# A new written order for the closing part of an RWKV-7 layer, with one more wait, and a few places changed in the order at the layer boundary

## The chip, the cores and the metric

The kernel runs on one core of one Trainium2 chip. A core has five engines with instruction queues of their own: TensorE (PE: matrix products into PSUM banks, and the loading of weights ahead of each, PEld), VectorE (DVE), ScalarE (ACT), GpSimd (POOL) and SyncE (SP), which here issues the DMA transfers. Engines wait for each other through semaphores; within an engine, instructions go in the order in which they were written into its queue. The metric is the device time of one execution in microseconds (us); lower is better. Times of before: 786.66, 784.89 and 787.54, with a median of 786.66.

## The reference, cut to what matters

One inference step of a two-layer decoder trunk with width 1024, run for a prompt of 512 tokens and for a sample group of 8 sequences of 4 tokens, 544 columns in all. Layer one mixes tokens with dilated windowed attention, layer two with RWKV-7 (12 heads of 64); each also attends to 256 memory tokens. The branches are joined, multiplied by a SiLU gate, and projected back to width 1024; the result is normalized (RMSNorm) and added to the layer's input. Of layer two:

```python
def mixer_b(xn, w_in, w_out, mu, w0, w_up, a0, a_up, k_k, k_a, r_k, ln_w, ln_b, mem_kv, shift_prev, s0):
    p = xn @ w_in
    cols = p[..., :C_SHIFT]
    ...
    xs = (cols + mu * (prev - cols)).astype(jnp.float32)
    w_log = -jax.nn.softplus(-(w0 + jnp.tanh(wd) @ w_up)) - 0.5
    decay = jnp.exp(-jnp.exp(w_log))
    a = jax.nn.sigmoid(a0 + ad @ a_up)
    ...
    y, S = wkv_scan(r, decay, k, v, -kk, kk * a, s0)
    mean = jnp.mean(y, axis=-1, keepdims=True)
    var = jnp.mean(jnp.square(y - mean), axis=-1, keepdims=True)
    y = (y - mean) * lax.rsqrt(var + GN_EPS) * ln_w.reshape(RWKV_HEADS, HEAD_DIM) + ln_b.reshape(RWKV_HEADS, HEAD_DIM)
    y = y + jnp.sum(r * k * r_k, axis=-1, keepdims=True) * v
    ...
    o_mem = cross_attn(q_mem, mem_kv)
    h = jnp.concatenate([y, o_mem], axis=-1) * jax.nn.silu(gate)
    return h @ w_out, cols[:, -1], S.astype(xn.dtype)
...
    sa = jnp.einsum('bhvk,bhk->bhv', S, a_t)
    S = S * w_t[:, :, None, :] + sa[..., None] * b_t[:, :, None, :] + v_t[..., None] * k_t[:, :, None, :]
    return S, jnp.einsum('bhvk,bhk->bhv', S, r_t)
...
        xp = xp + rms_norm(hp, norm_post[i])
        xs = xs + rms_norm(hs, norm_post[i])
```

The second function above is one step of the scan per head, and the last two lines stand around each layer. `r`, `k`, `v`, `wd` and `ad` are columns of `xs`. Beside the outputs of the trunk the kernel returns the new memory keys and values, rows of the windows, the states `S` and the shifted columns.

## The kernel before, in words

**Tiling.** All weights come from HBM in pieces of 256 KB. Products keep float32 accuracy by splitting each operand into a high and a low part and doing three matmuls for each product: high by high, high by low, low by high (L336 to L338 for input products, L1941 for output products). So each weight piece means one DMA issued on SP's queue, one cast on ACT for the high part (L328) and one subtraction on POOL for the low part (L329), ahead of its matmuls.

**The recurrence.** The 12 heads are handled as six pairs, and these as three groups of two pairs (g = 0, 1, 2). The 512 prompt tokens are cut into 8 chunks of 64. Within a chunk the recurrence needs the inverse of a triangular matrix. A forward elimination on DVE makes it for a group at once: 30 steps of two instructions each, a product (L1557) and an addition (L1559), on fewer columns from one step to the next. At two places (after steps 12 and 22) PE multiplies a finished square (L1541) and DVE copies it back, which the following steps need. A big transposition on DVE (L1569), two matmul groups on PE (X1 at L1579, X2 at L1589) and the products w (L1600) and q/v (L1615) then make the inputs of the chunks. The chunks of a group run one after another (class `Chunks`): `inputs` (PE with the state, then one DVE addition, L1795, then POOL scales the state, L1799) and `state` (PE, then one DVE addition that writes the new state St, L1812, or for the first a copy, L1814). Each such DVE instruction counts as one step of the chain; its number is kept in `n`, and the instructions in the list `ops`. `y_of` (L1757) makes the outputs y of two chunks in one PSUM bank: a first half (`e` is 1) without the two terms that depend on the second chunk's state, and a second half with the rest. [...]

**The closing part.** Up to some point, the order of all work comes from a planner (class `Flow`): each strand of work is a Python generator (a stream) with a rank, and `run` picks the stream to go on, by costs and due times. When the event "closing" comes, `close` (L231) takes over: it walks the string CLOSE (L57), and each word in it runs the named stream up to its next `yield`. This is done within a region with a manual schedule for PE, DVE, ACT and POOL: those four engines issue their instructions in the order written. SP's queue of DMA issues is not bound by it, nor is the place at which the first instructions of the region come among earlier ones on their engine. The streams are:

- F, `earlier`: the output projection of groups 0 and 1, two output halves each. Blocks of 128 tokens by 512 columns, six matmuls (L1941) in a PSUM bank from a pool of two that other work uses as well, then the addition to z on DVE (L2134). Block and addition are separate words, and the first words of a stream may only pass its events: counted from 0, F #3 is the first block that the list places and F #4 the first addition. A sample block (L1950, named o110s for group 1's second half) and its addition (zS, L2139) close each half. The blocks of group 1's second half are o110 t0 to t3.
- W: the weight pieces of these blocks and of group 2's.
- P2: the rest of the elimination of group 2, steps 8 to 30, the two squares (words P2 #6 and #17), transposition and products.
- W1: the group norm of group 1 held back until here: its matmul sums, POOL's statistics, the scaling yc (L1642, word #3), the matmul gn (L1648).
- R, `residuals` (L1983 to L2008): loads of x and of the norm's weights (R #2), then eight transposes of x on PE into the same pool of banks (L2001) with a copy on ACT (L2002), and the sample's (x1s).
- U, `inner`: the gating of group 1's heads (`gated`, k = 2, 3): one DVE instruction over 544 columns (L1929), casts on ACT (L1932), the low part on POOL (L1933).
- C, `chunks`: state and inputs of group 2's chunks; with the count of steps above there are 15 (state of chunk 0 is step 1, inputs 1 step 2, and so on).
- Y, `outputs` (its loop has `i` from 0 to 7): the calls of `y_of`. The stream yields at the events that it needs; a word is spent at each.
- N0 to N2: the group norms of the three blocks of y of group 2 (chunks 0 to 3, 4 and 5, 6 and 7; YB), with their gating; S2 and M2: the sample's chunk for group 2 (with the product q2s, L1682, and w2s and zs4 later) and its norm (M2 #1 is a power on POOL, L1640, and gn2s its matmul).
- O0 to O3, `last`: output blocks of group 2 for 128 tokens each (two blocks, additions, a square on ACT that sums up), the power on POOL, two products with the norm's weights (L2040, on POOL or DVE by the string MULT 'GGGGGGDD': POOL for O0 to O2, DVE for O3), two last additions of x with the store (L2045).
- L, `last_sample` (L2064 to L2078): the same for the sample, with a matmul sss (L2069) that sums over the partitions.

**The boundary.** Between layer one and layer two, the string PROGS (L35) gives by letters the order of PE's work in three patterns, each in a region with a manual schedule for PE alone (L1141): p is a part of layer one's last output product, P one of layer two's first products (L336 to L338), w and W are weight pieces of the output and of the memory, I the memory's input, r, a, A, b, B parts of the norm (powers and statistics), e early work, s sums of squares (ssz L1055, L1102), x loads of the layer's input, m memory keys and values, and k (`busy`, L1133) two matmuls of 128x128 whose result nobody reads, so PE only spends time with it.

Of the kernel before, what the change touches and what calls it, by code (L numbers as in the profile page):

```python
# [13 lines left out]
SYNC = DependencyInfo(DependencyClass.Sync, DependencyReason.DATA)  # L14
# [17 lines left out]
ET = mybir.EngineType  # L32
D, A, G = ET.DVE, ET.Activation, ET.Pool
MENG = set(), set(), set()
PROGS = ('xpxwpxpwpxPxwPwPsPxPxsxsWsswkPPWsWIPsWs', 'xrxxPWrPIsWxPrsWPrsxWaakxaPasabxsbIPxbaaaPPssbbIsbb', 'brermrkAArAmBBBAmBmABAmBmABmmAmBme')  # L35
LOP = (0, 3, 4)
WOB = 10
DU = 2
# [15 lines left out]
PRELOAD = ()  # L54
MULT = 'GGGGGGDD'
LOWER = 'GGGGGG'
CLOSE = 'F F F W1 W1 W1 P2 P2 P2 P2 F P2 P2 P2 F P2 R R F F W W P2 F F P2 F F P2 F F P2 P2 R W P2 W1 P2 R R F W1 W1 U U U W W P2 R F P2 F P2 U U P2 F P2 F P2 F F P2 W W F P2 F W F F R P2 F F P2 W W P2 F F P2 F F F P2 P2 F P2 P2 P2 P2 W W P2 F P2 P2 C C C F C C S2 S2 S2 F F Y Y Y Y C Y Y Y C W F C C Y Y W W F C Y Y Y N0 N0 C N0 F C F F Y Y Y N0 F C C Y Y Y N0 N1 N1 C F N0 N1 F C N0 N0 N1 F N1 C N1 Y Y Y F F N0 N0 N0 C C N1 N1 Y Y Y S2 N2 N2 O0 O0 O0 N1 N2 S2 O1 O1 O1 O0 N2 O1 S2 O0 N1 N1 S2 S2 O1 O0 O0 O1 S2 O2 O2 O2 S2 N2 O2 O1 O0 O0 S2 O2 O2 O0 O0 O1 O1 S2 S2 O1 O1 R M2 R N2 O2 N2 N2 R N2 R R N2 N2 M2 O2 O1 C O2 O0 O2 O2 M2 M2 L L L L O3 O3 O3 O3 O1 O1 O3 O3 L L O2 O2 O2 O3 O3 O3 L L O3 O3 L C C L L L O0 O0 O3 O3 O3 L L'  # L57
YB = [[[0, 4], [4, 8]], [[0, 4], [4, 8]], [[0, 4], [4, 6], [6, 8]]]
QUARTERS = (1, 1), (0, 0), (1, 0), (0, 1)
QO = (0, 2, 1, 3)  # L60
# [194 lines left out]
def _device(tc, I, O):  # L255
# [456 lines left out]
    with ExitStack() as pro:  # L712
# [44 lines left out]
        for j, g in enumerate(GORD):  # L757
            a = 1152 + 32 * j
# [259 lines left out]
    half = {}  # L1018
# [107 lines left out]
    def busy():  # L1126

        n = 0
        while True:
            pt = ps_q(f"busy{n}")  # L1130
            n += 1
            for _ in range(2):
# [7 lines left out]
             "e": early(), "k": busy(), "s": sums(), "x": x_in()}  # L1140
    for k, prog in enumerate(PROGS):  # L1141
        with tc.manual_schedule(engines={ET.PE} | MENG[k]) if MENG[k] is not None else ExitStack():
# [65 lines left out]
    flow = Flow(tc)  # L1208
# [97 lines left out]
    def turned(c, j, h):  # L1306
        return h ^ (c + j) % 2
# [438 lines left out]
    class Chunks:  # L1746

        def __init__(self, g):
            self.g, self.st = g, sts[g]
            self.states, self.c, self.yps, self.norms, self.fence, self.n, self.ops = [], 0, None, [], False, 0, []  # L1750
            self.St = rw.tile([128, 2, 64], F32, tag="St", bufs=4, name=f"St{g}i")
            nc.vector.memset(self.St, 0.0)
            self.states.append(self.St)
            self.zs = ps_zs(f"z{g}").rearrange("p (e k c v) -> p e k c v", k=2, c=4, v=64)
# [5 lines left out]
        def y_of(self, cs, e):  # L1760


            g, (AR, SR, UV, u) = self.g, (self.st.AR, self.st.SR, self.st.UV, self.st.u)
            a, b = [ab for ab in YB[g] if ab[0] <= cs[0] < ab[1]][0]
            if cs[0] == a and e:
                self.yps = ps_c("y", f"y{g}_{a}")
            yps = self.yps
            steps = [(c, k, t) for c in cs for k in range(3) for t in range(2) if (c or k) and (k == 0 and t) == e]
            for step in steps:
                c, k, t = step  # L1770
                for j, h in PAIRS:
                    if turned(c, j, h) == t:
                        r, s = score(c, j, h)
                        lhs = SR[r, 2 - k, j, s] if k else AR[H2[h], j, 1, CH[c]]
                        rhs = (UV[r, 1, j, unit(c, j, h)[1]] if k == 1 else u[r, c, t] if k else self.states[c][H2[h], j ^ h])
                        y = ((c - a) * 2 + h) * 64
                        self.put(yps[r, y:y + 64], lhs, rhs, e and step == steps[0], not e and step == steps[-1])
                        if not e and self.fence:
                            tc.add_manual_dep(flow.last(), self.ops[self.begun if g == 2 else -1].name, SYNC, reason="one half of a bank")
            c = cs[1]  # L1780
            if not e and c == b - 1:
                def out(pt):
                    pt = pt[:, 0:(b - a) * 128].rearrange("p (c j t) -> p c j t", j=2, t=64)
                    for j in range(2):
                        add_affine(2 * g + j, pt[:, :, j], slice(64 * a, 64 * b), True)

                self.norms.append(norm(g, yps, 2 * (b - a), f"_{b}", out, self.fence))
# [306 lines left out]
    def closing():  # L2094
# [65 lines left out]
        def outputs():  # L2160
            yield "chunks"
            C = out.chunks
            for i in range(8):
                c = i + 1
                yield f"step{2 * c - 2 + c % 2}"
                if i % 2:
                    yield f"step{n + 1}"
                else:
                    if [i] == [b for _, b in YB[2] if b == i]:
                        yield f"read{i}"  # L2170
                n = C.n
                if c % 2:
                    C.begun = n
                C.y_of((c - 1, c) if c % 2 else (c - 2, c - 1), c % 2 == 1)
                flow.done(f"turn{i}")
                yield
# [125 lines left out]
```

## Time and profile before

| | us |
|---|---|
| median of three runs | 786.66 |
| the profiled execution, its own time | 787.78 |
| its span, from the first to the last instruction | 785.9 |
| the first output block of the list CLOSE on PE (F #3) | starts at 690.03 |
| the second-level transposition on DVE (L1569) | starts at 714.55 |
| the last block-sized matmul on PE | ends at 775.57 |

The mean granted clock of TensorE in this execution is 0.986 of the full one. The page of the profile gives the busy time of each engine over the whole span and where the span's final chain ran. Its tables by stage (busy time in a stretch between two times, with the granted clock), the list of waits (engine, tile and line that waited, on what, the sum, how often, the longest) and single instructions in order of time (start, duration, engine, line, operation, out<-in; in brackets the idle time just before and what ended it) are where the numbers of the prediction come from. All starts are us from the first instruction of the span.

### The profile page before, as it was taken

The page shows a single profiled execution, that of the slowest core. Times are in us where ns is not written, and L with a number is a line of the kernel's source. Part 1 is how long each engine was busy: PE and PEld are TensorE (multiplying, and loading weights), DVE is VectorE, ACT ScalarE, POOL GpSimd, SP SyncE. Part 2 cuts the span into 40 slices and gives each one's busy share as a digit, 9 for nine tenths or more (in the row PEclk, how much of TensorE's full clock was granted, in tenths as well). Part 3 has the DMA queues.
Part 4 walks back from the last instruction along what each step waited for, and adds up shares of the span by engine and source line. Part 5 has one row for each costly group of instructions (what it writes and reads, how often), then busy time and mean ns, then how long its engine had stood idle before and what let it go on. Part 6 is the DMA issues. An engine that isn't in the chain of part 4 may idle for free.

```text
span 785.9 us, 20504 instructions
## 1 busy us (share of the span) xinstructions
PE 744.5 (95%) x8457; PEld 622.5 (79%) x8457; DVE 448.0 (57%) x1076; ACT 342.0 (44%) x807; POOL 354.4 (45%) x385
## 2 busy tenths in 40 slices
PE   6899999999999999999999999999999999989894
PEld 5877868888986877798888889888897888657763
DVE  7733321216646376662444679644799457777566
ACT  7554321214554364447585358223644242533122
POOL 4642322332240393655443338533855444333465
PEclk9999999999999999999999999899999999999997
DMA  7465358872133772263114522201222341622003
GB/s 254 126 204 200 108 172 278 318 279 98 63 116 117 250 233 75 69 198 103 54 49 148 166 80 80 71 16 33 80 73 83 112 112 56 185 93 84 17 15 132
DMA packets 58785, 98.21 MB, mean 125 GB/s; under 512 B 7775, under 2 KB 23039, under 8 KB 58655
## 3 DMA queue, kind: packets, MB, share of 16 engines
q1 hardware_dynamic: 58692, 96.91, 37.7%
q8 instruction: 66, 1.08, 0.6%
q14 instruction: 27, 0.22, 0.1%
HBM read 83.39 MB, written 13.49 MB: 123 GB/s over the span
## 4 chain that ended last, share of the span: by engine, by line
PE 67%; DVE 15%; POOL 5%; DMA 5%; ACT 3%; issue 3%; SPq 0%; DVEq 0%; POOLq 0%; ACTq 0%
PE o L1941 3%; PE Sx L591 2%; PE b_h L337 2%; PE y L1757 2%; PE b_h L336 2%; PE b_h L338 2%; DVE TX L1557 1%; PE z L1757 1%; PE sc L1473 1%; PE ox L615 1%; DMA raw_a<-in_w_in_a 1%; PE o L832 1%; PE ptx L607 1%; DVE T L1559 1%; PE w L1600 1%
## 5 line engine op out<-in xcount | busy, mean ns | idle before, releaser
L329 POOL TENSOR_TENSOR lo_a<-raw_a,hi_a 128x512 fp32r<-128x512 f32 x44 | 56.9, 1295 | 124.1 <-ACT hi_a L328 123.4
L329 POOL TENSOR_TENSOR lo_b<-raw_b,hi_b 128x512 fp32r<-128x512 f32 x58 | 78.5, 1354 | 73.4 <-ACT hi_b L328 62.4
L328 ACT CAST hi_a<-raw_a 128x512 fp32r<-128x512 f32 x44 | 27.3, 620 | 64.3 <-DMA raw_a<-in_w_in_a 36.5
L328 ACT CAST hi_b<-raw_b 128x512 fp32r<-128x512 f32 x58 | 36.4, 628 | 31.8 <-issue 9.9
L336 PE MATMUL b_h<-xg,hi_b 128*128 128x272 f32 x160 | 47.9, 300 | 0.0
L337 PE MATMUL b_h<-xg,lo_b 128*128 128x272 f32 x160 | 47.2, 296 | 0.0
L338 PE MATMUL b_h<-xg,hi_b 128*128 128x272 f32 x160 | 47.1, 295 | 0.0
L1941 PE MATMUL o<-hi_o,h 128*128 128x512 f32 x96 | 36.0, 426 | 2.9 <-DVE z L2134 2.3
L337 PEld LDWEIGHTS b_h<-xg,lo_b 128*128 128x128 f32 x160 | 30.1, 188 | 2.3 <-issue 1.9
L1559 DVE TENSOR_TENSOR T<-T,TX 128x30 f32<-128x30 f32 (+14 forms) x90 | 30.1, 335 | 2.2
L336 PEld LDWEIGHTS b_h<-xg,hi_b 128*128 128x128 f32 x160 | 30.1, 188 | 1.3 <-ACT hi_b L328 0.4
L1557 DVE TENSOR_TENSOR TX<-T,TT 128x30 f32<-128x30 f32 (+14 forms) x90 | 29.2, 325 | 3.3 <-ACT T L1528 1.7
L338 PEld LDWEIGHTS b_h<-xg,hi_b 128*128 128x128 f32 x160 | 30.1, 188 | 0.9 <-issue 0.5
L1941 PEld LDWEIGHTS o<-hi_o,h 128*128 128x128 f32 x96 | 18.8, 196 | 9.3 <-DVE z L2134 2.8
L329 POOL TENSOR_TENSOR lo_o<-raw_o,hi_o 128x512 fp32r<-128x512 f32 x12 | 15.7, 1316 | 22.1 <-ACT hi_o L328 14.8
L1799 POOL TENSOR_TENSOR Sd<-St,DF 128x128 f32<-128x128 f32 x21 | 8.9, 422 | 36.6 <-DVE St L1812 25.0
L1941 PE MATMUL o<-lo_o,h 128*128 128x512 f32 x48 | 19.7, 411 | 0.9 <-POOL lo_o L329 0.9
L1382 POOL TENSOR_TENSOR rv<-rv,mhalf 128x10 f32<-128x10 f32 x6 | 14.2, 2374 | 13.8 <-DVE rv L1381 7.7
L1473 PE MATMUL sc<-AR,BK 64*64 64x128 f32 x384 | 18.4, 278 | 1.9 <-DVE bv L1419 0.9
L824 ACT COPY PT<-pa 128x512 f32<-128x512 f32 x16 | 9.0, 586 | 18.7 <-PE pa L823 14.7
L1933 POOL TENSOR_TENSOR h<-ug,h 128x128 fp32r<-128x128 f32 (+3 forms) x11 | 9.1, 838 | 17.1 <-ACT h L1932 17.0
L1473 PEld LDWEIGHTS sc<-AR,BK 64*64 64x64 f32 x384 | 12.6, 132 | 5.2 <-issue 1.8
(1112 smaller groups left out, 2732.3 us busy)
## 6 DMA issues: line engine op xcount, KB each, us to landing
raw_b<-in_w_in_b SPq DMA_DIRECT2D x58, 256.0 KB, 2.9
raw_a<-in_w_in_a SPq DMA_DIRECT2D x44, 256.0 KB, 2.9
kc<-in_kc SPq DMA_DIRECT2D x18, 512.0 KB, 6.3
vc<-in_vc SPq DMA_DIRECT2D x18, 512.0 KB, 6.9
raw_o<-in_w_out_b SPq DMA_DIRECT2D x16, 256.0 KB, 2.6
out_win<-t SPq DMA_DIRECT2D x12, 272.0 KB, 3.4
x<-in_x SPq DMA_DIRECT2D x8, 272.0 KB, 5.2
xr<-in_x SPq DMA_DIRECT2D x16, 136.0 KB, 4.1
```

Source lines behind the costliest of these rows:

```text
L328: nc.scalar.copy(hi, raw)
L329: lo_eng.tensor_tensor(lo, raw, hi.bitcast(F32), ALU.subtract)
L336: nc.tensor.matmul(ps[:, :n], hi, xh, start=first, stop=False)
L337: nc.tensor.matmul(ps[:, :n], lo, xh, start=False, stop=False)
L338: nc.tensor.matmul(ps[:, :n], hi, xl, start=False, stop=last)
L591: nc.tensor.matmul(S[hh][64 * e:64 * e + 64, 0:256], qm[r, f, a:a + 64], kT[l][r, f, :], start=True, stop=True)
L1382: nc.gpsimd.tensor_tensor(rv[:, 1], rv[:, 0], mhalf.to_broadcast([128, 10]), ALU.pow)
L1473: nc.tensor.matmul(pts[e][unit(c, j, h)[0], a:a + 128], BK[H2[h], j, x, CH[c]], AR[H2[h], j, :, CH[c]], start=True, stop=True)
L1557: nc.vector.tensor_tensor(pd, TP[:, 0:s, s:s + 1].to_broadcast([128, s, w]), TT[:, s:s + 1, s + 1:32].to_broadcast([128, s, w]), ALU.mult)
L1559: nc.vector.tensor_tensor(TP[:, 0:s, s + 1:32], TP[:, 0:s, s + 1:32], pd, ALU.add)
L1757: nc.tensor.matmul(out, lhs, rhs, start=start, stop=stop)
L1941: nc.tensor.matmul(ps, x, w, start=begun is None and i + k == 0, stop=i == len(hs) - 1 and k == 2)
```

## The change

Three things are edited.

First, at the boundary the first pattern loses one k, and the second has three of them in place of one, with some of the letters x, r and s one place earlier or later.

Second, the list CLOSE is written anew. It holds the same words in another order, with three more words Y. The table gives some positions, counted in words from 0:

| what | before | after |
|---|---|---|
| first output block (F #3), first addition (F #4) | 2, 10 | 13, 16 |
| step 12 of the elimination, first square (P2 #5, #6) | 11, 12 | 8, 9 |
| second square (P2 #17), transposition (P2 #26) | 51, 79 | 40, 67 |
| the gatings k = 2 and k = 3 (U #3, #4) | 45, 54 | 72, 84 |
| first state update (C #3) | 101 | 93 |
| blocks o110 t0 to t3 (F #26, 28, 30, 32) | 75, 81, 84, 88 | 95, 100, 107, 110 |
| o110s (F #34) | 102 | 118 |
| q2s (S2 #3) | 107 | 23 |
| first halves of y | 112, 123, 141, 167 | 104, 122, 146, 169 |
| second halves of y | 116, 130, 148, 179 | 114, 129, 151, 181 |
| w2s (S2 #4), zs4 | 181, 189 | 183, 186 |
| power of the sample's norm (M2 #1), products of O2 | 228; 244, 246 | 242; 239, 240 |
| products of O3 | 269, 272 | 276, 281 |
| L #5, #7, #10 | 262, 270, 277 | 267, 269, 278 |

Third, first halves of y from the second on, y(2,3), wait as well: each of their matmuls waits for the first DVE step that comes after the second half before it was written (`ended` holds the count then). The stream Y yields once more ahead of each of these for the step after that one. For y(2,3) it is step 6 (inputs of chunk 3), for y(4,5) step 8, for y(6,7) step 12.

```diff
--- before.py
+++ after.py
@@ -32,7 +32,7 @@
 ET = mybir.EngineType
 D, A, G = ET.DVE, ET.Activation, ET.Pool
 MENG = set(), set(), set()
-PROGS = ('xpxwpxpwpxPxwPwPsPxPxsxsWsswkPPWsWIPsWs', 'xrxxPWrPIsWxPrsWPrsxWaakxaPasabxsbIPxbaaaPPssbbIsbb', 'brermrkAArAmBBBAmBmABAmBmABmmAmBme')
+PROGS = ('xpxwpxpwpxPxwPwPsPxPxsxsWsswPPWsWIPsWs', 'rxxPWrxPIskWxPksrWPrsxWaaaxaPasbkxsbIPxbaaaPPsbbIsbbs', 'brermrkAArAmBBBAmBmABAmBmABmmAmBme')
 LOP = (0, 3, 4)
 WOB = 10
 DU = 2
@@ -54,7 +54,7 @@
 PRELOAD = ()
 MULT = 'GGGGGGDD'
 LOWER = 'GGGGGG'
-CLOSE = 'F F F W1 W1 W1 P2 P2 P2 P2 F P2 P2 P2 F P2 R R F F W W P2 F F P2 F F P2 F F P2 P2 R W P2 W1 P2 R R F W1 W1 U U U W W P2 R F P2 F P2 U U P2 F P2 F P2 F F P2 W W F P2 F W F F R P2 F F P2 W W P2 F F P2 F F F P2 P2 F P2 P2 P2 P2 W W P2 F P2 P2 C C C F C C S2 S2 S2 F F Y Y Y Y C Y Y Y C W F C C Y Y W W F C Y Y Y N0 N0 C N0 F C F F Y Y Y N0 F C C Y Y Y N0 N1 N1 C F N0 N1 F C N0 N0 N1 F N1 C N1 Y Y Y F F N0 N0 N0 C C N1 N1 Y Y Y S2 N2 N2 O0 O0 O0 N1 N2 S2 O1 O1 O1 O0 N2 O1 S2 O0 N1 N1 S2 S2 O1 O0 O0 O1 S2 O2 O2 O2 S2 N2 O2 O1 O0 O0 S2 O2 O2 O0 O0 O1 O1 S2 S2 O1 O1 R M2 R N2 O2 N2 N2 R N2 R R N2 N2 M2 O2 O1 C O2 O0 O2 O2 M2 M2 L L L L O3 O3 O3 O3 O1 O1 O3 O3 L L O2 O2 O2 O3 O3 O3 L L O3 O3 L C C L L L O0 O0 O3 O3 O3 L L'
+CLOSE = 'R R W1 P2 P2 P2 P2 W1 P2 P2 P2 F F F P2 P2 F F P2 F P2 S2 S2 S2 R P2 R F P2 F R P2 F W1 P2 F P2 F W W P2 W P2 P2 F F P2 P2 W1 R R W1 W1 F P2 F P2 P2 W W P2 F R W W F R P2 F P2 U U U F F F P2 P2 F P2 W P2 P2 P2 U U P2 P2 P2 F F C C C F F F W W C F F Y Y Y Y C F C F F F C Y Y Y C C F W W Y Y Y W C F F Y Y Y C N0 N0 F F N0 C F N0 F C C F Y Y Y Y C N0 Y Y Y W W C N0 F N1 N1 F N0 N0 N1 C F F Y Y Y Y N1 C C F F N0 N0 N0 N1 Y Y Y S2 N2 N2 S2 R N1 N2 O0 O0 O0 N1 N1 N2 S2 N2 N1 N1 N1 R R O0 S2 O0 O0 N2 N2 N2 O2 O2 O2 S2 O0 O2 S2 O2 S2 O0 O0 N2 O0 O0 O0 N2 N2 O2 S2 O2 O1 O1 O1 O0 O0 O2 S2 S2 O1 O2 O2 O2 M2 O1 O1 C O1 O1 O1 O3 O3 O3 O2 M2 O3 M2 M2 L L L L O2 O2 O3 O1 O1 O3 L L L O3 O3 C C O1 L O3 L L L L O3 O3 O1 O1 O3 O3 O3 L L'
 YB = [[[0, 4], [4, 8]], [[0, 4], [4, 8]], [[0, 4], [4, 6], [6, 8]]]
 QUARTERS = (1, 1), (0, 0), (1, 0), (0, 1)
 QO = (0, 2, 1, 3)
@@ -1747,7 +1747,7 @@
 
         def __init__(self, g):
             self.g, self.st = g, sts[g]
-            self.states, self.c, self.yps, self.norms, self.fence, self.n, self.ops = [], 0, None, [], False, 0, []
+            self.states, self.c, self.yps, self.norms, self.fence, self.n, self.ops, self.ended = [], 0, None, [], False, 0, [], None
             self.St = rw.tile([128, 2, 64], F32, tag="St", bufs=4, name=f"St{g}i")
             nc.vector.memset(self.St, 0.0)
             self.states.append(self.St)
@@ -1775,8 +1775,9 @@
                         rhs = (UV[r, 1, j, unit(c, j, h)[1]] if k == 1 else u[r, c, t] if k else self.states[c][H2[h], j ^ h])
                         y = ((c - a) * 2 + h) * 64
                         self.put(yps[r, y:y + 64], lhs, rhs, e and step == steps[0], not e and step == steps[-1])
-                        if not e and self.fence:
-                            tc.add_manual_dep(flow.last(), self.ops[self.begun if g == 2 else -1].name, SYNC, reason="one half of a bank")
+                        if self.fence and not (e and self.ended is None):
+                            op = self.ops[(self.ended if e else self.begun) if g == 2 else -1]
+                            tc.add_manual_dep(flow.last(), op.name, SYNC, reason="one half of a bank")
             c = cs[1]
             if not e and c == b - 1:
                 def out(pt):
@@ -2165,7 +2166,9 @@
                 yield f"step{2 * c - 2 + c % 2}"
                 if i % 2:
                     yield f"step{n + 1}"
-                else:
+                elif i:
+                    yield f"step{n + 1}"
+                    C.ended = n
                     if [i] == [b for _, b in YB[2] if b == i]:
                         yield f"read{i}"
                 n = C.n
```

## The prediction

> **What bounds the kernel now.** I read the page first, then the table by stage, then what TensorE (PE) waited for, then VectorE (DVE) in order of time. From the page:
>
> ```profile
> span 785.9 us, 20504 instructions
> PE 744.5 (95%) x8457; PEld 622.5 (79%) x8457; DVE 448.0 (57%) x1076; ACT 342.0 (44%) x807; POOL 354.4 (45%) x385
> ```
>
> PE is busy 95% of the span, so on the whole a new order can win only what PE waits. The list CLOSE begins on PE with the first output block, at 690.03. I cut the rest into: until the second-level transposition of the elimination (714.55), until the first state update (728.30), the recurrence (until 751.23), the output stage (until the last block-sized matmul, 775.57), and the end. Busy time of each engine in these stretches (length, PE, PEld, DVE, ACT, POOL, then the granted clock):
>
> ```profile
> core 0: us, PE busy (x) PEld busy (x) DVE busy (x) ACT busy (x) POOL busy (x), PEclk, DMA share, GB/s
> 690.03:714.55 24.52, 20.81 (x160) 15.05 (x157) 21.02 (x55) 8.05 (x18) 12.14 (x11) 0.93 0.35 103
> 714.55:728.30 13.75, 13.72 (x358) 11.64 (x356) 8.79 (x10) 4.10 (x8) 3.15 (x4) 1.00 0.12 42
> 728.30:751.23 22.93, 20.23 (x453) 15.92 (x447) 13.87 (x39) 3.77 (x8) 9.76 (x14) 1.00 0.05 14
> 751.23:775.57 24.34, 23.38 (x270) 15.52 (x266) 17.67 (x42) 10.21 (x33) 18.29 (x20) 1.00 0.16 59
> 775.57:785.95 10.38, 0.59 (x3) 0.50 (x2) 4.69 (x10) 0.51 (x2) 3.37 (x5) 0.60 0.39 140
> ```
>
> PE idles 3.71, 0.03, 2.70 and 0.96 us, and the end costs 10.38 us with hardly a matmul: 7.4 us of idling are within reach of an order, and some of the end. What PE waited for in this part:
>
> ```profile
> PE o L1941 <- DVE z L2134: 2.3, 2, 1.6
> PE y L1757 <- DVE UV L1795: 1.4, 3, 0.5
> PE x L2001 <- ACT x1SA L2002: 0.7, 1, 0.7
> PE y L1757 <- DVE St L1812: 0.5, 1, 0.5
> PE o L1941 <- POOL lo_o L329: 0.4, 1, 0.4
> ```
>
> So the first stretch waits for DVE's additions (they free the two output banks), the recurrence for the DVE step ahead of each second half of y. DVE in order of time, around the start and at the end of the first stretch:
>
> ```profile
> 687.84 0.40 DVE L1559 TENSOR_TENSOR T<-T,TX 128x220 f32<-128x220 f32 x1
> 692.42 0.69 DVE L2134 TENSOR_TENSOR z<-z,o 128x512 f32<-128x512 f32 x1 [4.18 <-PE o L1941]
> 693.02 0.39 DVE L1557 TENSOR_TENSOR TX<-T,TT 128x228 f32<-128x228 f32 x1
> 693.45 0.40 DVE L1559 TENSOR_TENSOR T<-T,TX 128x228 f32<-128x228 f32 x1
> ...
> 714.55 2.09 DVE L1569 STREAM_TRANSPOSE TX<-T 128x1024 f32<-128x1024 f32 x1
> ```
>
> The reader should see that DVE stands 4.18 us after step 11, because the list puts the first addition (F #4) next and PE has not done its block, and that one later step (12) is 0.83 us, 693.02 to 693.85. From 692.42 to 714.55 are 22.13 us with little pause: this stretch is DVE's, while PE has free time.
>
> **The first stretch.** The new list puts steps 12 to 15 ahead of F #4, and the two gatings (U), two additions and one small addition behind the transposition. The groups of DVE in the stretch, and the chain's own durations of PE's pieces:
>
> ```profile
> L2134 DVE TENSOR_TENSOR z<-z,o 128x512 f32<-128x512 f32 x7 | 4.8, 681 | 4.3 <-PE o L1941 4.2
> L1929 DVE SCALAR_TENSOR_TENSOR ug<-bv,pv,ug 128x544 f32<-128x544 f32 x2 | 2.5, 1248 | 0.0
> ```
>
> ```profile
> 733.28 1.59 PE o L1941 x6
> 728.38 1.01 PE o110s L1950 x32
> 730.54 0.34 PE q2s L1682 x8
> 768.49 0.66 PE x L2001 x4
> ```
>
> Out of DVE's stretch go 4 steps (4 x 0.83 = 3.3, into the 4.18 us of idling), two gatings (2.5), two additions (1.4) and a small one (0.3): 7.5. Into it come the scaling yc of W1 #3, which stood ahead of step 8, a small copy behind q2s (0.3), and pauses where a bank is not yet done (0.4). What yc costs depends on GpSimd (POOL):
>
> ```profile
> 683.34 1.77 DVE L1642 TENSOR_TENSOR yc<-yc,gst 128x512 f32<-128x512 f32 x1 [0.78 <-POOL gst L1640]
> 742.69 0.88 DVE L1642 TENSOR_TENSOR yc<-yc,gst 128x512 f32<-128x512 f32 x1
> ```
>
> ```profile
> 683.28 2.97 POOL L329 TENSOR_TENSOR lo_o<-raw_o,hi_o 128x512 fp32r<-128x512 f32 x2
> ```
>
> The same operation is 1.77 beside a weight piece on POOL and 0.88 without. In the new list the pieces W #1 and W #3 stand five to eight entries behind yc, so I take 1.3, from bounds 0.88 and 1.77. [...] Out minus in is 7.5 - 2.0 = 5.5: the transposition at about 709.0.
>
> PE has then done less. Four blocks (o110 t0 to t3, 1.59 each, 6.4) are pushed behind the first state update; two transposes of x (0.66 each) and q2s (0.34) come ahead of it, 1.7. From the transposition to the state update the products are the same; PE first waits out the 2.09 of the transposition, and one block and the sample product (1.59 + 1.01) stand where two blocks stood (3.2), with some 0.5 of waiting for copies: 13.6 as against 13.75. So the state update comes 5.6 earlier with 4.7 more to do: a gain of 0.9.
>
> Against this stands the clock. Three equal windows around 705.94:
>
> ```profile
> 702.52:705.94 3.42, 1.19 (x14) 0.71 (x13) 3.35 (x9) 1.28 (x4) 0.43 (x1) 1.00 0.30 81
> 705.94:709.35 3.41, 3.40 (x8) 2.72 (x9) 3.22 (x7) 1.13 (x4) 2.15 (x2) 0.50 0.34 85
> 709.35:712.76 3.41, 3.38 (x42) 2.57 (x42) 3.24 (x9) 0.91 (x3) 2.60 (x2) 1.00 0.47 124
> ```
>
> After a window with PE busy 1.19 of 3.42 the granted clock is 0.50 for one window, where 8 matmuls took 3.4 instead of 2.1 (six are 1.59). Before, DVE set the pace there and this cost nearly nothing. In the new order PE again stands, between the second square (P2 #17) and the seventh transposition of x (R #7), about 2 us in a window of 3.4, so it may happen again and then delay F #16, on which the last addition before the transposition waits: between 0 and 1.3, of which I take 0.4. Net gain here 0.5. [...]
>
> The moved pieces W each issue a DMA on SP's queue, a cast on ScalarE and a subtraction on POOL, and R #2 issues its loads before the first block; SP is not bound by the list. Each piece is still written several blocks ahead of its use; were one late, the nearest row is the 0.4 of lo_o above.
>
> **The added wait.** From the third step on, the first half of y now waits for the DVE step that follows the last second half, too. On PE the state product and all later blocks queue behind it, and DVE's next St waits for these. For y(2,3) this is the step of inputs 3: o110s (1.01) stands between it and y in the list, against a round trip of 0.4 to 0.5 (the y rows above). For y(4,5) it is inputs 4, for y(6,7) inputs 6, with later steps and blocks between. I cost it at 0; without o110s it is 0.5, once.
>
> **The recurrence.** Before, 2.70 idle: 1.9 at the four second halves of y (1.4 + 0.5), the rest elsewhere. In the new list blocks stand between inputs and state nearly throughout, and the second half of y(0,1) follows two blocks after its step. Three second halves still have their step right ahead of them (state 3, state 5, inputs 7): 3 x 0.45 = 1.35, and state 6 queues on DVE behind a norm's statistics, 0.4. Gain 2.70 - 1.75 = 0.95.
>
> **Output stage and end.** PE loses two transposes (1.3) and gains half a group of norm transposes (0.4). Idle was 0.96. Now zs4 follows w2s directly and waits for its copy (0.35); and the sample norm's power M2 #1 stands on POOL behind both products of O2:
>
> ```profile
> 765.76 2.50 POOL L2040 TENSOR_TENSOR z<-z,post 128x512 f32<-128x512 f32 x2
> 768.41 0.54 POOL L1640 TENSOR_TENSOR gst2s<-gst2s,mhalf 128x1 f32<-128x1 f32 x1
> ...
> 771.99 2.99 POOL L2040 TENSOR_TENSOR z<-z,post 128x512 f32<-128x512 f32 x2
> ```
>
> Two products are 2.5 to 3.0. Walking POOL from the second UX on, the power comes some 1.8 us after its input, of which O1's second block and state 7 hide all but about 0.95. Gain 0.9 + 0.96 - 1.3 = 0.55. At the end:
>
> ```profile
> 777.78 0.60 PE sss L2069 x2
> ...
> 779.14 0.74 DVE z L2045
> ```
>
> The last sum (sss) comes about 0.5 sooner after the last block, since zS is added before the products, but one product of O3 (as long as an addition, 0.68) now stands behind it among the last y: 0.2 lost.
>
> **The boundary.** The filler (k) goes once from the first pattern and comes twice more in the second, with some sums and powers exchanged:
>
> ```profile
> 294.50 0.64 PE busy L1133 x4
> ```
>
> ```profile
> PE ssz L1055 <- ACT sqoo L1037: 1.9, 4, 0.8
> ```
>
> Each filler is 0.64. The one removed stands between busy matmuls; of the new ones, two take the place of waits for ACT, and the third stands ahead of one. Bounds -1.3 and +1.3; I take -0.3.
>
> **Sum.** -0.5 - 0.95 - 0.55 + 0.2 - 0.3 = -2.1, which I cut to -1.8, since durations without POOL beside them flatter DVE. The profiled execution is 787.78 (its span 785.9): 786.0. From the median, 786.66: **784.9**. About 0.3%, 2.4 us, is what a measurement of this kernel can tell from no change, so this counts as the same, not far from its edge. Chance 0.37.
>
> **Rivals.** *No half clock and no wait for POOL*: the 0.4 and the 0.95 fall away, and the fillers cost nothing (0.6): -3.75, 782.9. [...] Chance 0.33. *The list does not bind the place of the first square*: its matmul (P2 #6) has been ready long, but may be queued behind all earlier output products, until 690; DVE's copy of it then stops steps 13 to 15 (2.5) until 690.4, F #4 slips to 693.1, and 0.7 is lost: 785.6, the same. Chance 0.17. *POOL in the output stage* (slower): POOL is busy 18.29 of 24.34 there. The power M2 #1 has both products of O2 ahead of it, and O1's second product stands ahead of the power of O3. It decides once O2's statistics come over 1 us later than I walk them; then PE stands for two products and a power before gn2s (2.99 + 0.54) and the last y for another product (1.5): 784.9 + 5.0 = 789.9. Chance 0.13.
>
> Faster by over 0.3%: the first rival and a little of the forecast, 0.38; within: 0.49; slower: 0.13. The range runs from 1.9 below the first rival, for the boundary and the cover of the lists, to 1.0 below the slow one: 781.0 to 788.9.
>
> **What would show it.** Right: DVE without the 4.18 pause, the transposition some 5.5 us sooner after the first block, no idle over 0.1 before the first halves of y, three waits of 0.4 to 0.5 before second halves, and PE waiting near gn2s. Wrong: a first square after 690, a window at clock 0.50 that delays the transposition, a wait before y(2,3), or a longer end.

## The result and the profile after

The changed kernel takes 781.75 (779.06 to 782.5 in five runs) against 786.66 of the kernel before: a ratio of 0.9934, with a 95% interval of 0.9916 to 0.9952. In a later run (after_again) it was 0.9904 (0.9877 to 0.9932). So it is faster by about 5 us or somewhat more, against the 1.8 of the forecast. The profiled execution is the fastest of its five runs, 779.06 with a span of 777.4; the spans of the other four are 780.0 to 780.8. From the page of the changed kernel:

```profile
span 777.4 us, 20495 instructions
PE 739.6 (95%) x8461; PEld 619.2 (80%) x8461; DVE 443.8 (57%) x1076; ACT 342.7 (44%) x807; POOL 353.2 (45%) x385
```

One correction to the text above: in names like F #3, P2 #6 or M2 #1 the words of a stream are counted from 1, not from 0 (positions in the list are counted from 0). The lines of the changed kernel's code are one to three higher behind the edit: the output blocks are L1942, the additions L2135.

Where the time went is read from the table by stage, over the whole kernel this time: the boundary (from the first ssz to the first b18h), from there to the first kn of group 2, from there to the list's first block F #3 (called the middle below), to the big transposition, to the first state update, to the last sample product o21s, to the end. The kernel before, as far as not shown:

```profile
288.34:324.34 36.00, 33.57 (x261) 24.83 (x261) 22.84 (x58) 21.25 (x54) 22.62 (x29) 1.00 0.34 105
324.34:503.28 178.94, 175.45 (x1664) 154.97 (x1661) 106.64 (x285) 103.73 (x261) 90.92 (x102) 1.00 0.32 102
503.28:690.03 186.75, 181.56 (x2677) 155.79 (x2678) 121.60 (x301) 72.69 (x165) 88.42 (x94) 0.98 0.28 84
...
714.55:728.61 14.06, 14.03 (x370) 11.94 (x372) 9.10 (x12) 4.41 (x8) 3.46 (x4) 1.00 0.12 41
728.61:775.57 46.96, 43.29 (x711) 31.13 (x700) 31.22 (x80) 13.68 (x41) 27.74 (x34) 1.00 0.11 37
```

The changed kernel, the same stretches:

```profile
287.27:323.02 35.75, 34.18 (x265) 25.41 (x265) 23.61 (x57) 20.67 (x53) 22.41 (x29) 1.00 0.33 106
323.02:501.96 178.94, 175.45 (x1664) 154.95 (x1661) 107.09 (x286) 103.74 (x261) 91.36 (x103) 1.00 0.33 102
501.96:682.80 180.84, 179.78 (x2685) 155.02 (x2686) 115.51 (x299) 72.99 (x165) 88.08 (x96) 0.98 0.29 87
682.80:703.54 20.74, 15.34 (x120) 11.12 (x116) 18.69 (x54) 7.01 (x15) 6.62 (x5) 1.00 0.27 71
703.54:717.27 13.73, 13.20 (x384) 11.33 (x383) 9.39 (x13) 5.81 (x13) 5.83 (x6) 1.00 0.25 70
717.27:767.19 49.92, 47.42 (x720) 34.26 (x720) 32.24 (x83) 13.85 (x40) 30.95 (x38) 1.00 0.16 51
767.19:777.37 10.18, 0.38 (x2) 0.30 (x2) 4.60 (x9) 0.51 (x2) 2.62 (x3) 0.70 0.34 118
```

The two profiled spans differ by 8.6, more than the medians (4.9): that of before lies above its median, and that of the changed kernel is its fastest. Of the 8.6 the boundary is 0.25 (36.00 to 35.75), and the list in its four stretches 1.35: 3.78 and 0.33 gained up to the first state update, 2.96 given back behind it, 0.20 gained at the end. Before the boundary lie 1.07 (a window at half clock, 30.11 to 33.52 at a granted clock of 0.50, in the one and not in the other, nothing that the change touches). The rest, 5.91, is the middle, 186.75 to 180.84, of which no line of the diff speaks. Both executions have two windows at half clock there, each 3.41 long at a granted clock of 0.50 (504.56 to 511.38 before, 600.52 to 607.35 now).

In the middle PE's order of work has changed. In it neither kernel has a manual schedule for any engine: the order of issue is made when the program is built, not written. PE's order is the same in both from the boundary's end to 504; then it parts. PE in order of time, the kernel before and then the changed one:

```profile
505.37 0.59 PE L336 MATMUL b4h<-xg,hi_b 128*128 128x272 f32 x1
...
506.67 0.43 PE L338 MATMUL b4h<-xg,hi_b 128*128 128x272 f32 x1
507.03 0.47 PE L1600 MATMUL w<-SA,UV 64*64 64x64 f32 x2
```

```profile
503.74 0.39 PE L336 MATMUL b4h<-xg,hi_b 128*128 128x272 f32 x1
...
504.96 0.29 PE L336 MATMUL b4h<-xg,hi_b 128*128 128x272 f32 x1
505.18 0.32 PE L1600 MATMUL w<-SA,UV 64*64 64x64 f32 x2
```

Before, six matmuls of the input product b4h stand ahead of the first w, now ten; from there to the list much of the work stands in another order. The work itself is the same but for the first square (eight matmuls), which now falls into the middle. PE is not alone in this: the order of VectorE parts near 324, that of ScalarE and POOL near 513 and 517 (times of before); only the order of SP's DMA issues is unchanged. What PE waits for in the middle, before and then changed, largest first (left out is a wait of 0.9 for the first kn, in both, which ends where the stretch begins):

```profile
PE o00s L1950 <- ACT z L1970: 1.0, 1, 1.0
PE b5h L336 <- DVE TX L1557: 0.7, 1, 0.7
PE sc L1473 <- DVE SR L1481: 0.7, 1, 0.7
PE sc L1473 <- DVE bv L1419: 0.6, 1, 0.6
```

```profile
PE sc L1473 <- DVE SR L1481: 0.7, 2, 0.4
PE b17h L336 <- DVE xr L1221: 0.2, 1, 0.2
```

PE idles 5.19 of the middle before (186.75 less 181.56 busy) and 1.06 now. So 4.1 of the 5.9 are waits that are gone; the other 1.8 are PE's busy time. By tile, the products w are busy for 6.01 before and 4.45 now, those of b4h for 9.51 and 7.60, while others take a little more. Before, the two windows at half clock fall on w and b4h (504.55 to 511.38), so part of this is where the windows lie (one matmul of w takes 0.22 to 0.37 before and 0.22 to 0.27 now).

### The profile page after: what moved, and what is told of

Same layout as the page of the kernel before. It is cut to its first block, busy times and chain, and to the rows that moved or that the text cites. A ratio compares the mean times of both kernels' runs of the same rounds, so it can differ in the third digit from the quotient of the medians.

```text
span 777.4 us, 20495 instructions
## 1 busy us (share of the span) xinstructions
PE 739.6 (95%) x8461; PEld 619.2 (80%) x8461; DVE 443.8 (57%) x1076; ACT 342.7 (44%) x807; POOL 353.2 (45%) x385
## 4 chain that ended last, share of the span: by engine, by line
PE 74%; DVE 12%; ACT 4%; POOL 3%; issue 3%; DMA 2%; SPq 1%; DVEq 0%; ACTq 0%; POOLq 0%
PE o L1942 4%; PE b_h L336 2%; PE b_h L338 2%; PE y L1757 2%; PE b_h L337 2%; PE Sx L591 2%; PE sc L1473 2%; PE z L1757 2%; DVE T L1559 1%; DVE TX L1557 1%; PE o L832 1%; PE ox L615 1%; PE ptx L607 1%; PE ssz L1055 1%; PE pa L823 1%
## 5 line engine op out<-in xcount | busy, mean ns | idle before, releaser
L1942 PE MATMUL o<-hi_o,h 128*128 128x512 f32 x96 | 35.9, 418 | 1.5 <-ACT x1BK L2003 1.2
L336 PEld LDWEIGHTS b_h<-xg,hi_b 128*128 128x128 f32 x160 | 31.0, 194 | 2.8 <-issue 1.3
L338 PEld LDWEIGHTS b_h<-xg,hi_b 128*128 128x128 f32 x160 | 30.8, 193 | 0.3
L1942 PEld LDWEIGHTS o<-hi_o,h 128*128 128x128 f32 x96 | 18.0, 188 | 7.1 <-ACT x1BK L2003 1.4
L1942 PE MATMUL o<-lo_o,h 128*128 128x512 f32 x48 | 19.0, 397 | 0.6 <-POOL lo_o L329 0.6
L1796 DVE TENSOR_TENSOR UV<-z,UV 128x128 f32<-128x128 f32 x21 | 6.1, 289 | 18.8 <-PE z L1757 18.6
```

What stands on the lines that cost most here:

```text
L336: nc.tensor.matmul(ps[:, :n], hi, xh, start=first, stop=False)
L338: nc.tensor.matmul(ps[:, :n], hi, xl, start=False, stop=last)
L1942: nc.tensor.matmul(ps, x, w, start=begun is None and i + k == 0, stop=i == len(hs) - 1 and k == 2)
```

## The experiments

The theory was that the boundary's letters act mainly through this later order of PE (no run changes the order of one engine alone, so what is tested is the order of all four together), and that the list is worth little more than its own stretches show; the rivals, that the list or the boundary's own waits carry the gain. Ratios are against the kernel before on the same chip; the middle is read from each trace, with the number of windows at half clock in it.

| run | ratio | 95% interval | middle | half-clock windows in it |
|---|---|---|---|---|
| changed kernel | 0.9934 | 0.9916 to 0.9952 | 180.84 | 2 |
| after_again | 0.9904 | 0.9877 to 0.9932 | 179.54 | 1 |
| list_only | 0.9974 | 0.9958 to 0.9990 | 188.15 | 2 |
| progs_only | 0.9929 | 0.9913 to 0.9945 | 179.92 | 1 |
| new_filler_26 | 0.9919 | 0.9896 to 0.9941 | 178.41 | 0 |
| new_filler_20 | 0.9956 | 0.9939 to 0.9972 | 177.98 | 0 |
| moves_undone | 0.9908 | 0.9877 to 0.9940 | 181.10 | 2 |
| oldb_filler_17 | 0.9947 | 0.9930 to 0.9965 | 181.52 | 0 |
| oldb_filler_10 | 0.9989 | 0.9969 to 1.0009 | 179.07 | 0 |
| wait_only | 1.0011 | 0.9992 to 1.0030 | 187.36 | 2 |
| m2_between | 0.9931 | 0.9906 to 0.9956 | 179.83 | 1 |
| yc2s_early | 0.9927 | 0.9903 to 0.9952 | 179.62 | 1 |
| first_back | 0.9943 | 0.9919 to 0.9967 | 181.42 | 2 |

**The changed kernel again: after_again.**

> The changed kernel once more, beside the other three of this call on one chip. Expected: 781.7 within 1.5, and in the trace the stretch from the first kn to the list's first block at 178.4 plus 1.2 to 1.5 for each window at half clock in it.

779.81, 0.4 below the expected range (on this chip the kernel before is at 788.11), and the middle close to what was expected: 179.54 with one window at half clock, 1.1 above 178.41. So the reading of the table's last two columns holds.

**The list alone: list_only.** PROGS as before, all else as changed.

> The new list CLOSE with its wait, the boundary's patterns as before. Between the boundary and the list (on PE from 503 to the list's first block) PE's order of work is then the one of before. Theory: the change's gain came mostly from that middle part, which nothing in the diff names: in the two profiled executions the stretch from the first kn of group 2's inputs to the list's first output block went from 186.75 to 180.84, the list itself only from 95.87 to 94.60, the boundary's stretch from 40.36 to 40.10. So this kernel should be at about 786.66 - 1.3 = 785.4, with the middle at 186 to 187. Rival (the list is the cause, by another way than its own stretch): about 782. Rival (the boundary's own waits): 786.4.

785.06, a gain of 1.3 by the medians on its chip (786.35 before) and of 2.0 by the ratio, against the 1.3 expected; the rival's 782 is out. PE's order up to the first square, near 673, is that of before. By stage, the middle and the stretch from F #3 to the transposition; and VectorE at the list's start:

```profile
504.28:692.43 188.15, 182.19 (x2686) 156.03 (x2686) 123.28 (x309) 72.99 (x166) 88.75 (x96) 0.98 0.28 83
692.43:711.68 19.25, 15.20 (x120) 11.14 (x116) 15.01 (x43) 6.69 (x14) 6.71 (x5) 1.00 0.28 85
```

```profile
694.81 0.69 DVE L2135 TENSOR_TENSOR z<-z,o 128x512 f32<-128x512 f32 x1 [3.82 <-PE o L1942]
```

The transposition comes 5.27 sooner after F #3 (24.52 to 19.25), as the prediction had it (5.5). But VectorE still stands 3.82 ahead of the first addition: steps 12 to 15 run ahead of the pause, not in it. And the middle is 1.4 longer (186.75 to 188.15; 186 to 187 was expected): ahead of F #3, PE waits 1.2 for a weight's low part on POOL instead of 0.4, and the first square now lies in it. From F #3 to the end list_only takes 93.00, before 95.92; net of the 1.4 the list is worth 1.5.

**The boundary alone: progs_only.** PROGS as changed, all else as before.

> The boundary's new patterns, with the list and the waits of before. PE's order in the middle of layer two is then the one of the changed kernel. Theory (middle part): about 781.75 + 1.3 = 783.0, with the middle stretch at about 181. Rival (the list): 786.3, with the middle at about 186. Rival (the boundary's own waits, without the middle): 783, but with the gain in the stretch from 287 to 328, not in the middle.

781.31 (783.0 was expected): the whole gain of the change without its list. The middle and the closing part:

```profile
503.88:683.80 179.92, 178.35 (x2678) 153.69 (x2678) 115.59 (x298) 72.85 (x165) 87.44 (x94) 0.99 0.29 88
683.80:779.51 95.71, 78.40 (x1230) 58.33 (x1226) 67.19 (x158) 26.83 (x68) 46.71 (x52) 0.95 0.21 65
```

The middle is the changed kernel's, the closing part (95.71) that of before (95.92). The boundary's stretch is 35.52, 0.5 shorter; so the gain is not there. What the list adds on top, 1.1 by these stretches (94.57 in the changed kernel), the ratios don't resolve (0.9929 against 0.9934 and 0.9904).

**A filler that leaves the order, and one that doesn't: new_filler_26, new_filler_20.** The changed kernel with one more k, of work that nobody needs:

```diff
-'brermrkAArAmBBBAmBmABAmBmABmmAmBme'
+'brermrkAArAmBBBAmBmABAmBmAkBmmAmBme'
```

> The changed kernel with one more filler (k) late in the third pattern, at a place where PE's later order stays as in the changed kernel. Theory: the filler itself costs between 0 and 0.64, so 781.8 to 782.4, with the middle at about 181. Any larger loss would mean that the boundary's own stretch is worth more than its rows show.

780.4, below the expected 781.8 to 782.4, with the middle in the changed kernel's order and at 178.41, without a window at half clock. The filler costs nothing that can be measured: the stretch that it stands in takes 179.00, in the changed kernel 178.94.

```diff
-'brermrkAArAmBBBAmBmABAmBmABmmAmBme'
+'brermrkAArAmBBBAmBmAkBAmBmABmmAmBme'
```

> The changed kernel with one more filler in the third pattern, six letters earlier: the same cost in the boundary, but PE's order in the middle of layer two comes out as a third one, neither that of before nor that of the changed kernel. Theory (the middle's order carries the gain): the time differs from the run with the later filler by the difference of their middle stretches, anywhere from -1 to +5, so 781 to 787. Rival (the boundary's own waits or the list): the same as the run with the later filler within 0.5, 781.8 to 782.4.

782.5, with a third order. It is slower than the other filler by 0.0037, some 2.9 us (the intervals just touch), though the two do the same work at the boundary; but not by its middle, which is no longer (177.98; ten matmuls of bk, which in the other run belong to the middle, stand behind F #3 here). So the theory's "by the difference of their middle stretches" falls. The loss lies at the list's start:

```profile
681.49:705.44 23.95, 18.32 (x129) 13.27 (x126) 20.45 (x60) 7.45 (x17) 6.37 (x5) 0.86 0.21 58
```

```profile
PE x L2002 <- DVE z L2135: 2.7, 2, 2.5
```

From F #3 to the transposition it takes 23.95 (the other filler 20.75): PE reaches the list with VectorE further behind (step 11 begins 1.76 after F #3, in the other run 0.17 before it), waits 2.5 in one piece for the first addition, and then has two windows at half clock. So the order of the middle also decides where each engine stands when the list begins. How much of the 3.2 it costs is not separated: two such windows cost this stretch 2.1 in the changed order as well (22.86 in yc2s_early).

**The moved letters: moves_undone.**

```diff
-'rxxPWrxPIskWxPksrWPrsxWaaaxaPasbkxsbIPxbaaaPPsbbIsbbs'
+'xrxxPWrPIskWxPksrWPrsxWaaaxaPasbkxsbIPxbaaaPPssbbIsbb'
```

> The changed kernel with the letters x and the last letters s of the boundary's second pattern back in their old places; the fillers stay as changed. PE's order in the middle of layer two is then that of the changed kernel. Theory (of the boundary only the order that it brings about later counts): the changed kernel's time within 0.5, the middle as there. Rival (the moved loads and sums were worth something of their own): slower by 0.5 to 1.3, seen in the boundary's stretch (35.75 from the first ssz to the first b18h in the changed kernel).

0.9908 beside 0.9904 of the changed kernel on the same chip (779.0 against 779.81; within 0.5 was expected), the same order in the middle, the boundary 35.50 against 35.67. The moved loads and the last sums are worth nothing that shows; what remains of the boundary's edit is the fillers (one fewer in the first pattern, two more and their places in the second), with one r and s exchanged and one a earlier.

**The old boundary with a filler: oldb_filler_17, oldb_filler_10.** The list as changed, the first two patterns as before, one k in the third:

```diff
-'brermrkAArAmBBBAmBmABAmBmABmmAmBme'
+'brermrkAArAmBBBAmkBmABAmBmABmmAmBme'
```

> The new list with the boundary's first two patterns as before, and one filler more in the third pattern, at a place where PE's later order in the middle of layer two comes out as another one than in any kernel so far. Theory (the middle's order carries the gain, and the order of before was a poor one): its middle stretch falls from 188.15 (the run with the new list alone) towards 178 to 182, so 778 to 782, although nothing of the change is made in the boundary and a filler only adds work. Rival (the changed letters of the boundary carry it): 785 to 786, the run with the new list alone plus 0 to 0.6.

```diff
-'brermrkAArAmBBBAmBmABAmBmABmmAmBme'
+'brermrkAArkAmBBBAmBmABAmBmABmmAmBme'
```

> The same with the filler at an earlier place in the third pattern, which gives yet another order of PE in the middle of layer two. Theory: the middle falls outside 186 to 188 again, either way, and the time goes with it, one for one at the same number of windows of half clock. Rival: 785 to 786.

The first gives 0.9947, a gain of about 4 with none of the changed letters (list_only has 0.9974; the intervals overlap a little): the middle falls to 181.52, still 3 above the changed order's 178.41. Neither has a window at half clock in it; list_only's 188.15 has two, so of its 6.6 more some 2.2 to 3.0 are the windows (1.1 to 1.5 each, see below) and the rest the order. The theory's range was 778 to 782, and it came out at 783.1. The second missed: 0.9989, although its middle fell to 179.07. The stretch ahead of it grew; in the other kernels that one takes 178.9 to 179.4. By stage, and PE's waits in it:

```profile
324.32:508.27 183.95, 177.46 (x1668) 156.90 (x1665) 106.75 (x285) 104.01 (x261) 90.98 (x102) 0.99 0.30 99
```

```profile
PE spare L439 <- DVE mvT L433: 2.9, 2, 2.3
PE busy L1133 <- DVE z L1062: 1.2, 1, 1.2
```

The filler is not free at this place: it waits 1.2 for its bank, the tile mvT of the memory part comes late from VectorE behind it (2.3 in one piece, 0.5 in list_only), and a window at half clock follows, near 344 us. Together the two stretches take 363.0, in list_only 367.1, in the changed kernel 359.8. So this execution is still ahead of list_only's when the list begins, and loses that again in the list: from F #3 to the end 97.16 against 93.00, with two windows at half clock in it (at 696.00 and 750.61) where list_only has none before the end. How much of that falls in its other executions is not known. "One for one" with the middle fell here as well.

**The added wait alone: wait_only.** The old list with three more words Y, and the edit of y_of.

> The kernel of before, its boundary and its list in their old order, with the added wait alone (three more words Y in the list, each right ahead of a first half of y, which then waits for the next DVE step). The prediction has the wait at 0: then the time is that of before within 0.5 (785.9 to 786.9), and no wait over 0.1 stands ahead of the second, third or fourth first half of y. Rival (the wait costs a round trip where nothing lies between): 0.4 to 0.5 for each of up to three, 786.8 to 787.9.

787.79 beside 787.22 on its chip (785.9 to 786.9 was expected, from 786.66), the same; by the interval alone (up to 1.0030) the rival's 1.2 would still fit. The trace decides: from the first state update to o21s it is 46.96, before 46.97, and PE's waits for y are those of before:

```profile
PE y L1757 <- DVE UV L1796: 1.4, 3, 0.5
...
PE y L1757 <- DVE St L1813: 0.5, 1, 0.5
```

The wait costs nothing even without the new order. Second halves of y in the last group wait in every kernel here (`fence`, for the first DVE step behind the first half): what either wait guards against, no run shows.

**POOL and the sample's norm: m2_between, yc2s_early.** In the changed kernel PE waits 0.72 ahead of gn2s, where the prediction had 0.95 and named POOL. One word moved:

```diff
-S2 S2 O1 O2 O2 O2 M2 O1 O1 C O1 O1 O1 O3 O3 O3 O2 M2 O3 M2
+S2 S2 O1 O2 M2 O2 O2 O1 O1 C O1 O1 O1 O3 O3 O3 O2 M2 O3 M2
```

> The changed kernel with one word of its list moved: the sample norm's power goes between the two products of O2 on POOL, instead of behind both; PE, DVE and ACT keep their order. Theory (POOL's queue costs PE there, predicted 0.95, in the trace of the changed kernel 0.72 ahead of gn2s): that wait falls under 0.1, and the time by 0.4 to 0.7, to about 781.1. Rival (the wait only moves to the next sum or to the products behind): 781.75, with the same sum of PE's waits from the last UX to the end.

VectorE, and then PE:

```profile
766.33 0.28 DVE L1813 TENSOR_TENSOR St<-z,Sd 128x128 f32<-128x128 f32 x1
767.26 0.29 DVE L2036 SCALAR_TENSOR_TENSOR rvt<-rvt 128x1 f32<-128x1 f32 x1 [0.65 <-ACT sq L2034]
767.48 0.74 DVE L2046 SCALAR_TENSOR_TENSOR z<-z,rvt,x1BK 128x512 f32<-128x512 f32 x1
768.14 0.21 DVE L1642 TENSOR_TENSOR yc2s<-yc2s,gst2s 128x64 f32<-128x64 f32 x1
```

```profile
768.50 0.33 PE L1651 MATMUL gn2s<-ident,yc2s 64*64 64x64 f32 x4 [0.83 <-DVE yc2s L1642]
```

The power is done at 766.27 on POOL, and yc2s starts at 768.14 all the same: it stands behind O1's small sum and O2's addition. The wait stays; POOL was not the cause. The time, 781.69, is the rival's. So VectorE's word was moved ahead of these two as well:

```diff
-S2 S2 O1 O2 O2 O2 M2 O1 O1 C O1 O1 O1 O3 O3 O3 O2 M2 O3 M2
+S2 S2 O1 O2 M2 O2 O2 O1 O1 C M2 O1 O1 O1 O3 O3 O3 O2 O3 M2
```

> The changed kernel with the sample norm's power between O2's products on POOL, as in the run m2_between, and the scaling yc2s on VectorE moved ahead of O1's small sum and O2's addition, behind the last St. In m2_between POOL did the power earlier, but PE's wait ahead of gn2s stayed at 0.8, and yc2s stood on VectorE behind those two, of which the first waited 0.65 for ScalarE. Theory (VectorE's order, not POOL, holds gn2s): the wait falls under 0.1 and the end comes 0.5 to 0.8 sooner after the first state update than in the changed kernel. Rival (yc2s has another wait of its own): still 0.6 or more ahead of gn2s.

VectorE, POOL and PE:

```profile
762.03 1.07 DVE L1642 TENSOR_TENSOR yc2s<-yc2s,gst2s 128x64 f32<-128x64 f32 x1
```

```profile
761.74 1.28 POOL L2041 TENSOR_TENSOR z<-z,post 128x512 f32<-128x512 f32 x1
```

```profile
763.25 0.33 PE L1651 MATMUL gn2s<-ident,yc2s 64*64 64x64 f32 x4
...
765.86 0.42 PE L1951 MATMUL o20s<-w2h,xsm 128*32 128x128 f32 x8 [0.68 <-ACT xsm L1932]
```

The wait ahead of gn2s is gone, as the theory had it, but no time is gained: PE now waits 0.68 ahead of o20s, one step down the same chain, and from the first state update to o21s it is 50.18 instead of 49.92. The end did not come sooner.

**The first stretch: first_back.** F #3 and F #4 ahead of step 12:

```diff
-R R W1 P2 P2 P2 P2 W1 P2 P2 P2 F F F P2 P2 F F P2 F
+R R W1 P2 P2 P2 P2 W1 F F F F P2 P2 P2 P2 P2 F P2 F
```

> The changed kernel with the first output block and the first addition (F #3, F #4) put back ahead of step 12 of the elimination. Theory (VectorE's chain sets the first stretch): VectorE stands some 3 us ahead of that addition, the big transposition comes 2.5 to 3.4 later after the first block than the changed kernel's 20.7, and PE, which has no blocks left there to do, waits nearly as much: 784 to 785. Rival (PE's work in this stretch covers it): the transposition later, but the end within 0.7 of the changed kernel, 781.7 to 782.4.

782.67 against 779.81 of after_again on the same chip, slower by 0.0039, about 3 us (the intervals overlap a little). The profiled execution is the slowest of twelve, 787.89. The stretch and VectorE's pause:

```profile
686.40:710.80 24.40, 18.38 (x127) 13.10 (x124) 18.95 (x54) 6.99 (x15) 6.95 (x7) 0.86 0.21 59
```

```profile
688.92 0.69 DVE L2135 TENSOR_TENSOR z<-z,o 128x512 f32<-128x512 f32 x1 [1.89 <-PE o L1942]
```

The transposition is 3.66 later after F #3 than in the changed kernel. VectorE's own pause is 1.89, less than the 3 expected; the rest comes with two windows at half clock in this stretch, which cost it 2.1 in the changed order too. So about 1.5 of the 3.66 are VectorE's, less than the theory's 2.5 to 3.4. The time is longer by about what the theory gave; how much of that is the order of the list's start and how much half clock is not shown, since the windows come and go.

No version beats the changed kernel by more than the intervals.

## Why the prediction was right, and where it failed

The time lies in the range, close to the first rival's 782.9, but not for that rival's reasons: the wait near gn2s was there, and half clock came and went. That the range holds it is luck in the main: the sum's terms for what the change names were about right, and most of the gain comes from a term that it did not have.

- **What an order can win.** The prediction said that a new order can win only what PE waits, and looked for it in the boundary and in the list alone. The step that failed is the tacit one between: that an order that is not written stays as it was. Between the boundary and the list the sum has no term. There PE's idle time fell from 5.19 to 1.06, and the middle by 5.9.
- **The first stretch.** Predicted: the transposition 5.5 sooner and the state update 5.6 sooner after F #3. In list_only they come 5.3 and 5.6 sooner; in the changed kernel 3.8 and 4.1, since PE reaches the list earlier there and VectorE does not. The 4.18 pause is absent in the changed kernel, but list_only shows that the reason given (steps 12 to 15 fill it) was wrong. yc took 0.68, below both bounds of 0.88 and 1.77. Half clock was put at 0 to 1.3, and 0.4 taken. Six executions have the changed list up to here and the changed order ahead of it (yc2s_early with a small difference): three without a window take 20.74 or 20.75 from F #3 to the transposition, after_again with one 21.81, and two with two 22.86 and 22.88. So a window costs 1.1 here, and two cost more than the list gains as a whole (1.35).
- **What comes behind.** By the prediction's terms 3.2 (4.7 - 0.95 - 0.55) is given back; measured 2.96. Of the waits in the recurrence 1.75 were to be left. PE's waits from the first state update to o21s in the changed kernel:

```profile
PE y L1757 <- DVE St L1813: 1.0, 2, 0.5
PE gn2s L1651 <- DVE yc2s L1642: 0.7, 1, 0.7
PE y L1757 <- DVE UV L1796: 0.4, 1, 0.4
PE zs L1699 <- DVE AR L1684: 0.3, 1, 0.3
```

  Three second halves wait 0.4 to 0.5 each, as said, and zs4 0.3. The 0.7 at gn2s has the predicted size and the wrong cause: VectorE's order, not POOL's.
- **The end**: 0.2 sooner instead of 0.2 later; the sum sss waits 1.4 instead of 2.2. **The added wait**: 0, shown by wait_only. **The boundary's own stretch**: 0.25 against 0.3.
- **The rivals.** The first square, which the second rival had at 690 or later, starts on PE at 676.83: the list does not bind its place, but it went earlier. The slow one, POOL in the output stage, did not come about.

What stays open: why a filler at one place reorders the work 200 us later and at another does not. That the build orders by estimated times would explain it, but is only argued. Which engine's new order takes the waits away was not separated, nor how much of the 1.8 of busy time is the order and how much the place of the half-clock windows.

## What to carry to other kernels

Where an engine's order is not written, compare it over the whole program before and after a change: an edit in one place may move work in another, and the gain may lie there. Give a change's local stretches and the rest separate lines in the sum. A wait that is taken away from one step of a chain may stand ahead of the next one (the 0.7 at gn2s came back as 0.68 at o20s), so an edit is judged by the stretch's length and not by the wait.

## What the runs showed of the hardware

**Half clock.** Executions in the same order differ by where windows of 3.41 at half clock (granted clock 0.50) fall. The middle in the changed order takes 178.41 with none, 179.54 to 179.92 with one, 180.84 to 181.42 with two: 1.1 to 1.5 for each. At the list's start such a window follows one in which PE was busy for 0.77 (first_back) to 2.02 (yc2s_early) of 3.41, but that alone is no rule. The run new_filler_20, and then the changed kernel at two places:

```profile
684.71:688.12 3.41, 0.90 (x11) 0.30 (x9) 3.24 (x10) 0.20 (x1) 0.00 (x0) 1.00 0.41 127
688.12:691.54 3.42, 2.34 (x9) 1.54 (x9) 3.28 (x10) 1.01 (x3) 0.00 (x0) 0.50 0.00 0
```

```profile
597.11:600.52 3.41, 2.75 (x69) 2.21 (x70) 3.20 (x13) 0.27 (x2) 2.67 (x4) 1.00 0.46 141
600.52:603.94 3.42, 3.42 (x24) 2.58 (x23) 3.32 (x8) 0.02 (x1) 1.78 (x2) 0.50 0.25 92
...
685.86:689.27 3.41, 2.18 (x19) 1.36 (x18) 3.27 (x9) 0.00 (x0) 0.00 (x0) 1.00 0.44 139
689.27:692.69 3.42, 2.24 (x14) 1.65 (x11) 2.29 (x7) 1.33 (x3) 0.00 (x0) 1.00 0.00 0
```

After 0.90 and after 2.75 busy of 3.41 the next window is at 0.50; after 2.18 it is at full clock. So windows with work in them, even much of it, were followed by half clock; what decides where half clock falls is not shown.

**A scaling beside POOL.** In yc2s_early the small scaling takes 1.07 (762.03 to 763.10) instead of the 0.21 of m2_between, and ends 0.08 after the POOL product of 128x512 beside it (761.74 to 763.02). It is not so beside every POOL instruction: in the changed kernel the same scaling takes 0.22 (762.84 to 763.06) while POOL works at a power of 128x1 (762.33 to 763.33). What makes the difference was not tested.
